# RMSNorm with Swish: the second load goes out from ScalarE's queue beside the first, and gamma's transfer goes behind it

## The chip, the cores and the metric

The kernel runs on one core of a Trainium2 chip. The metric is the device time of one execution in microseconds (us). Most executions of one kernel agree within 0.3%.

A core has 16 DMA engines, which move data between HBM and the on-chip memory. Kernels ask for transfers through queues; this kernel uses two, one issued by SyncE (SP) and one by ScalarE (ACT). In the profile, "SPq" and "ACTq" are the sequencers of those two engines, which issue the transfers; "ACT", "DVE" and "POOL" are the compute engines ScalarE, VectorE and GpSimd.

## The reference

```python
# x: (16, 1024, 512) float32, gamma: (512,), eps = 1e-5
def reference(x, gamma, eps):
    rms = np.sqrt(np.mean(x ** 2, axis=-1, keepdims=True) + eps)
    x_norm = x / rms * gamma
    return (x_norm * (1.0 / (1.0 + np.exp(-x_norm)))).astype(np.float32)
```

That is 16,384 rows of 512 numbers, 33.55 MB in and 33.55 MB out, and little arithmetic for each.

## The kernel before

The rows are cut into tiles of `sz` times 128 rows: each of the 128 partitions takes `sz` rows that lie one after another in HBM, so each partition's part of a load is one contiguous piece of `sz` × 2 KB. The tiles sit in a ring of 96 row slots (25 MB), are worked on in place in chunks of 4 slots, and are stored from there. "Load 0" is the load of the first tile (4 slots, 1 MB), "load 1" the second (4), "load 2" the third (8), "load 3" and later ones 16.

```python
sizes = [4, 4, 8] + [16] * 6 + [8, 8]
ring = 96
ahead = 32
cn = 4
# ...
def load(t):
    nc.sync.dma_start(out=buf(t), in_=dram(xf, t))

def store(t):
    nc.scalar.dma_start(out=dram(of, t), in_=buf(t))
# ... sums(k): squares summed, 3 rows of a chunk on ScalarE, 1 on VectorE
# ... root(k): VectorE, then a power on GpSimd; norm(k): 4 VectorE instructions; swish(k): Silu on ScalarE

with tc.manual_schedule():
    nc.gpsimd.memset(gamma4[:], 0.0)
    nc.gpsimd.memset(neg_half[:], -0.5)
    nc.scalar.dma_start(out=gamma4[0:P:32, :], in_=gamma.partition_broadcast(4))
    nc.scalar.preload_act_table_set("silu_and_others")

    loaded = 0
    rows_loaded = 0
    while rows_loaded < ahead:
        load(loaded)
        rows_loaded += tiles[loaded][1]
        loaded += 1
    # ...
    for k in range(K + 3):
        if k < K:
            sums(k)
            root(k)
        while stored < len(tiles) and ends[stored] <= k - 2:
            store(stored)
            stored += 1
        if k == 0:
            nc.vector.stream_shuffle(gamma_sb[:], gamma4[:], [0] * 32)
        if 1 <= k <= K:
            norm(k - 1)
        if 2 <= k < K + 2:
            swish(k - 2)
            # ... further loads
```

## Time and profile before

| | before |
|---|---|
| time, median | 163.01 us (162.89 to 163.02) |
| span in the profile | 161.1 us |
| moved by DMA | 67.15 MB, 417 GB/s over the span |
| the two queues' packets, share of 16 engines | 49.1% + 48.4% |
| VectorE / ScalarE busy | 69% / 74% |
| ScalarE waits for data, whole run | 23.9 us |

These lines of the page of the kernel before give busy times in us, the DMA total, and the share of the 16 DMA engines' time that each queue's packets took (q1 is SyncE's queue of loads, q10 ScalarE's of stores and gamma):

```profile
DVE 110.7 (69%) x226; ACT 118.7 (74%) x225; POOL 46.4 (29%) x38
DMA packets 3180, 67.15 MB, mean 417 GB/s; under 512 B 356, under 2 KB 356, under 8 KB 360
q1 hardware_dynamic: 1584, 33.56, 49.1%
q10 hardware_dynamic: 1592, 33.56, 48.4%
```

No compute engine is busy as much as three quarters of the time; together the DMA queues are busy 97.5% of it. An average can mix stages, so the windows view of the kernel before is worth a look. Its columns are the stretch, its length, busy time of DVE, ACT and POOL with instruction counts, the clock, the DMA share, and GB/s. A packet, which is one piece that a DMA engine moves at a time, is counted in the stretch in which it starts, so a share can exceed 1:

```profile
0.00:2.00 2.00, 0.00 (x0) 0.00 (x0) 0.77 (x6) 1.00 0.20 25
2.00:3.00 1.00, 0.00 (x0) 0.60 (x1) 0.00 (x0) 1.00 0.62 213
3.00:8.00 5.00, 1.18 (x5) 2.63 (x7) 0.16 (x1) 1.00 1.01 428
8.00:24.00 16.00, 11.03 (x23) 9.62 (x21) 5.17 (x4) 1.00 1.03 431
24.00:100.00 76.00, 67.99 (x140) 72.67 (x140) 28.77 (x20) 1.00 1.00 430
100.00:150.00 50.00, 30.48 (x61) 33.13 (x58) 11.52 (x8) 1.00 1.00 431
150.00:158.00 8.00, 0.00 (x0) 0.00 (x0) 0.00 (x0) 1.00 1.01 432
158.00:161.00 3.00, 0.00 (x0) 0.00 (x0) 0.00 (x0) 1.00 0.13 55
```

From 3 us to 158 us the engines are full, at the same 430 GB/s whether they only load (up to about 20 us), load and store, or only store (the last stretch). Only the first 3 us and the last 3 us have idle DMA time. The compute columns tell the other half: after 150 us nothing computes at all, and stores still drain.

The timeline view of the kernel before shows the start. Its columns are start, length, engine, line and operation, and in brackets the idle time before it and what ended that:

```profile
0.74 23.23 SPq L70 DMA_DIRECT2D xb<-in_x_dram  x8
1.29 1.08 ACTq L116 DMA_DIRECT2D gamma<-in_gamma_dram  x1
...
5.54 0.63 ACT L80 ACTIVATE junk_a<-xb 128x512 bf16<-128x512 f32 x1 [1.85 <-DMA xb<-in_x_dram]
...
8.09 0.63 ACT L80 ACTIVATE junk_a<-xb 128x512 bf16<-128x512 f32 x1 [0.60 <-DMA xb<-in_x_dram]
...
12.98 0.63 ACT L80 ACTIVATE junk_a<-xb 128x512 bf16<-128x512 f32 x1 [2.94 <-DMA xb<-in_x_dram]
...
14.83 1.89 ACT L111 ACTIVATE xb<-xb 128x2048 f32<-128x2048 f32 x1
...
23.70 0.63 ACT L80 ACTIVATE junk_a<-xb 128x512 bf16<-128x512 f32 x1 [3.34 <-DMA xb<-in_x_dram]
```

Loads 0, 1, 2 and 3 reach ScalarE at 5.54, 8.09, 12.98 and 23.70 us, and each time ScalarE was already waiting. Compute is ahead of the data.

### The profile page before, as it was taken

How to read it: one execution, taken by the hardware profiler on the slowest of the kernel's cores; microseconds unless marked ns; L12 is line 12 of the kernel's file. 1: busy time of each engine (PE TensorE's matmuls, PEld its weight loads, DVE VectorE, ACT ScalarE, POOL GpSimd, SP SyncE). 2: the span in 40 equal slices, each digit the busy share in tenths (PEclk: the TensorE clock that was granted, in tenths of full speed). 3: DMA queues.
4: the chain of work that ended last, by engine and by line, in shares of the span. 5: the costliest groups of instructions: out<-in, count | busy, mean ns of one | idle time of the engine just before them, and what ended most of it. 6: DMA issues, size and time to landing. Idle time of an engine off the chain costs nothing.

```text
span 161.1 us, 612 instructions
## 1 busy us (share of the span) xinstructions
DVE 110.7 (69%) x226; ACT 118.7 (74%) x225; POOL 46.4 (29%) x38
## 2 busy tenths in 40 slices
DVE  0376946998999999999966998069999604990000
ACT  3447919999999999999939996099999408954000
POOL 1052403333444433333333333033333302400000
DMA  5999989999899999999999999999999999999993
GB/s 171 437 435 521 390 352 488 413 403 480 366 407 431 484 411 447 399 456 447 399 447 456 399 439 464 417 415 421 431 435 464 419 403 472 415 415 423 439 415 146
DMA packets 3180, 67.15 MB, mean 417 GB/s; under 512 B 356, under 2 KB 356, under 8 KB 360
## 3 DMA queue, kind: packets, MB, share of 16 engines
q1 hardware_dynamic: 1584, 33.56, 49.1%
q10 hardware_dynamic: 1592, 33.56, 48.4%
q14 instruction: 4, 0.03, 0.0%
HBM read 33.56 MB, written 33.55 MB: 417 GB/s over the span
## 4 chain that ended last, share of the span: by engine, by line
DMA 59%; ACT 20%; another core or an unknown queue 4%; issue 4%; DVE 3%; SPq 1%; DVEq 0%; ACTq 0%
DMA xb<-in_x_dram 41%; DMA out_dram<-xb 19%; ACT junk_a L80 12%; ACT xb L111 8%; DVE xb L104 3%; SPq L70 1%; DVEq L178 0%; DVE aeps L93 0%; ACTq L80 0%
## 5 line engine op out<-in xcount | busy, mean ns | idle before, releaser
L104 DVE SCALAR_TENSOR_TENSOR xb<-xb,rstd,gamma_sb 128x512 f32<-128x512 f32 x128 | 87.4, 745 | 0.0
L80 ACT ACTIVATE junk_a<-xb 128x512 bf16<-128x512 f32 x96 | 59.0, 615 | 23.9 <-DMA xb<-in_x_dram 23.9
L97 POOL TENSOR_TENSOR rstd<-aeps,neg_half 128x4 f32<-128x4 f32 x32 | 45.6, 1426 | 94.1 <-DVE aeps L93 94.1
L111 ACT ACTIVATE xb<-xb 128x2048 f32<-128x2048 f32 x32 | 60.7, 1896 | 1.8 <-DVE xb L104 1.8
L86 DVE CUSTOM_DVE_ANT_0 junk_v<-xb 128x512 bf16<-128x512 f32 x32 | 21.9, 685 | 19.6 <-DMA xb<-in_x_dram 19.6
L80 ACT ACTIVATION_READ_ACCUMULATOR junk_a<-xb 128x1 f32 x96 | 18.0, 187 | 0.0
L93 DVE TENSOR_SCALAR aeps<-ms 128x4 f32<-128x4 f32 x32 | 5.4, 170 | 14.5 <-ACT junk_a L80 14.5
L117 ACT ACT_TABLE_LOAD x1 | 1.3, 1283 | 2.4 <-issue 2.4
L86 DVE DVE_READ_ACCUMULATOR2_ANT ms<- 128x1 f32 x32 | 2.6, 82 | 0.0
L140 DVE STREAM_SHUFFLE gamma_sb<-gamma 128x512 f32<-128x512 f32 x1 | 0.7, 725 | 0.0
L114 POOL MEMSET gamma<- 128x512 f32 x1 | 0.5, 524 | 0.3 <-POOLq L164 0.3
L164 POOL MEMSET const-float32-0.0<- 128x1 f32 x1 | 0.1, 98 | 0.2 <-issue 0.2
L164 POOL MEMSET const-bfloat16-1.0<- 128x1 bf16 x1 | 0.1, 101 | 0.0
L164 POOL MEMSET const-uint8-127<- 128x1 uint8 x1 | 0.1, 101 | 0.0
L115 POOL MEMSET neg_half<- 128x4 f32 x1 | 0.1, 101 | 0.0
L164 POOL MEMSET const-float32-1.0<- 128x1 f32 x1 | 0.1, 98 | 0.0
L140 DVE LOAD_MASK_SELECT gamma_sb<-gamma x1 | 0.0, 14 | 0.0
## 6 DMA issues: line engine op xcount, KB each, us to landing
xb<-in_x_dram SPq DMA_DIRECT2D x6, 4096.0 KB, 43.8
out_dram<-xb ACTq DMA_DIRECT2D x6, 4096.0 KB, 34.6
xb<-in_x_dram SPq DMA_DIRECT2D x3, 2048.0 KB, 38.8
out_dram<-xb ACTq DMA_DIRECT2D x3, 2048.0 KB, 13.9
xb<-in_x_dram SPq DMA_DIRECT2D x2, 1024.0 KB, 5.8
out_dram<-xb ACTq DMA_DIRECT2D x2, 1024.0 KB, 19.7
gamma<-in_gamma_dram ACTq DMA_DIRECT2D x1, 8.0 KB
```

Source lines behind the costliest of these rows:

```text
L70: nc.sync.dma_start(out=buf(t), in_=dram(xf, t))
L80: nc.scalar.activation(out=junk[:], in_=row, func=AF.Square, accum_out=ms[:, k, j : j + 1],)
L86: nc.vector.tensor_tensor_reduce(out=junk[:], in0=row, in1=row, scale=1.0, scalar=0.0, op0=ALU.mult, op1=ALU.add, accum_out=ms[:, k, j : j ...
L93: nc.vector.tensor_scalar(out=aeps[:, k, :], in0=ms[:, k, :], scalar1=inv_d, scalar2=eps_f, op0=ALU.mult, op1=ALU.add,)
L97: nc.gpsimd.tensor_tensor(out=rstd[:, k, :], in0=aeps[:, k, :], in1=neg_half[:], op=ALU.pow)
L104: nc.vector.scalar_tensor_tensor(out=row, in0=row, scalar=rstd[:, k, j : j + 1], in1=gamma_sb[:], op0=ALU.mult, op1=ALU.mult,)
L111: nc.scalar.activation(out=rows, in_=rows, func=AF.Silu)
L114: nc.gpsimd.memset(gamma4[:], 0.0)
L115: nc.gpsimd.memset(neg_half[:], -0.5)
L117: nc.scalar.preload_act_table_set("silu_and_others")
L140: nc.vector.stream_shuffle(gamma_sb[:], gamma4[:], [0] * 32)
L164: nc = _bacc.Bacc("TRN2", target_bir_lowering=False, num_devices=1)
```

## The change

The intent is to have two loads under way from the start: SyncE and ScalarE each issue one at the same moment, instead of SyncE issuing both in turn while ScalarE waits for a memset so that it can fetch gamma.

```diff
     def load(t):
-        nc.sync.dma_start(out=buf(t), in_=dram(xf, t))
+        queue = nc.scalar if t == 1 else nc.sync
+        queue.dma_start(out=buf(t), in_=dram(xf, t))
@@
         nc.gpsimd.memset(neg_half[:], -0.5)
-        nc.scalar.dma_start(out=gamma4[0:P:32, :], in_=gamma.partition_broadcast(4))
-        nc.scalar.preload_act_table_set("silu_and_others")
@@
             load(loaded)
             rows_loaded += tiles[loaded][1]
             loaded += 1
+        nc.scalar.dma_start(out=gamma4[0:P:32, :], in_=gamma.partition_broadcast(4))
+        nc.scalar.preload_act_table_set("silu_and_others")
```

## The prediction

> **What bounds the kernel.** The DMA engines. The page counts 67.15 MB moved in a span of 161.1 us. The two hardware queues are busy 49.1% + 48.4% of 16 engines' span, 157.1 us, so 427 GB/s while busy. VectorE is busy 69%, ScalarE 74%. The windows of every 10 us from 24 to 150 us show a DMA share of 0.97 to 1.05; only the first 2.8 us and the last 3 us (share 0.35, then 0.04) are not full. The last store is issued at 146.8 us and lands 13.5 us later, behind a backlog of stores, so compute has several us of slack at the end as well.
>
> **What the change does.** SyncE issues load 0 at 0.74 us (0.37 us), load 1 at 1.16 (0.42), load 2 at 1.63 (0.42). ScalarE issues gamma at 1.29 us (1.09 us), because it waits for GpSimd's memset of that tile, which ends at 1.25; the table load follows at 2.40. After the change, ScalarE should issue load 1 at about 0.74 us, beside load 0, and still reach gamma at about 1.3 and the table load at about 2.4. Load 2 leaves SyncE about 0.45 us earlier. No bytes are added or removed.
>
> The Trainium skill ("DMA: Bandwidth & Descriptors", sections "Issuing engines are not separate DMA queues" and "Queues, rings and completion order") says that both queues run on the same 16 engines, which alternate between them by packet, and that a second issuer saves only issue time. The trace agrees so far: it never holds more than about 430 GB/s with one queue or two. So loads 0 and 1 should not land at about 5.5 and 8.1 us but both near 7.8 us, and gamma just after.
>
> **The critical path, step by step.**
> 1. Start-up: the first packets run from 1.63 us and the engines are full from about 2.8 us. Load 0's issue, which starts this, does not move. Load 1 0.4 us earlier fills nothing, because load 0's packets are not yet through. Worth 0 to -0.3 us; if two simultaneous issues hinder each other, 0 to +0.3.
> 2. First compute: ScalarE's first sum moves from 5.54 to about 7.8 us. Chunk 1's sums then follow chunk 0's without the 0.6 us wait.
> 3. Recovery: before, ScalarE idled 2.94 us until 12.98, for load 2. Cumulative bytes until then are the same, so load 2 still lands near 12.9. Working through VectorE's order with its durations (sum 0.69, shuffle 0.72, four norms 2.73) and the power on GpSimd (1.0 to 1.4), the first norms end near 14.7 rather than 12.9, and the first Silu starts at 14.8 to 15.3 instead of 14.83. Whatever is left is absorbed by the 3.3 us wait for load 3 (23.70 us).
> 4. Load pacing: completion semaphores are reused in program order, so gamma's later place makes SyncE's sixth load wait for load 1, the seventh for load 2 and the eighth for gamma: issued near 8, 13 and 13 us instead of 5.5, 8.0 and 23.6. SyncE's queue holds over 8 MB throughout, so this moves no byte.
>
> So a delay of about 2.3 us for the first data, all off the critical path; net about -0.1 us.
>
> **Prediction:** 162.9 us, range 162.4 to 163.6. Faster by over 2%: 0.01; within 2%: 0.98; slower: 0.01.
>
> **What would show it right:** ScalarE's first sum at 7.5 to 8.1 us; load 2 and load 3 first used at 13.0 and 23.7, within 0.3; last loads first used near 133.7; mean rate 417 GB/s again. **Wrong if** load 0 still lands near 5.5 us (the queues are not shared evenly), if the DMA windows before 3 us differ clearly, or if a store leaves so late that a DMA window drops below 0.9.

## The result, and the profile after

The changed kernel takes 163.13 us (median of 4 executions, 163.06 to 163.27), the kernel before 163.01. The ratio is 1.001, with a 95% interval of 0.9993 to 1.0027: the same. Here and below, a ratio is the mean time of one kernel's runs over the mean of the other's in the same rounds, so it is not quite the ratio of the medians quoted. Executions over 1.5% slower than the fastest of the same kernel are left out of the means.

These are the same lines of the page after the change:

```profile
DVE 110.6 (69%) x226; ACT 118.6 (74%) x225; POOL 46.4 (29%) x38
DMA packets 3180, 67.15 MB, mean 416 GB/s; under 512 B 356, under 2 KB 356, under 8 KB 360
q10 hardware_dynamic: 1736, 34.61, 50.0%
q1 hardware_dynamic: 1440, 32.51, 47.6%
```

One megabyte has moved from q1 to q10; the sum is the same. The timeline view after the change:

```profile
0.74 0.41 ACTq L71 DMA_DIRECT2D xb<-in_x_dram  x1
0.74 23.08 SPq L71 DMA_DIRECT2D xb<-in_x_dram  x7
1.29 1.08 ACTq L124 DMA_DIRECT2D gamma<-in_gamma_dram  x1
...
8.01 0.63 ACT L81 ACTIVATE junk_a<-xb 128x512 bf16<-128x512 f32 x1 [4.33 <-DMA xb<-in_x_dram]
...
13.04 0.63 ACT L81 ACTIVATE junk_a<-xb 128x512 bf16<-128x512 f32 x1 [1.25 <-DMA xb<-in_x_dram]
...
14.89 1.89 ACT L112 ACTIVATE xb<-xb 128x2048 f32<-128x2048 f32 x1
...
23.56 0.63 ACT L81 ACTIVATE junk_a<-xb 128x512 bf16<-128x512 f32 x1 [3.13 <-DMA xb<-in_x_dram]
```

Both first loads are indeed issued at 0.74 us. The first sum then starts 2.47 us *later* than before (8.01 against 5.54), because two transfers that share the engines both finish when the second would have. That delay is gone six microseconds later: load 2 is in use at 13.04 us (12.98 before), the first Silu starts at 14.89 (14.83), load 3 is in use at 23.56 (23.70). It was taken out of ScalarE's wait for load 2, which shrinks from 2.94 to 1.25 us, and out of the idle gap between chunks 0 and 1.

The windows view after the change, for the stretches in which it could differ:

```profile
0.00:2.00 2.00, 0.00 (x0) 0.00 (x0) 0.77 (x6) 1.00 0.37 66
2.00:3.00 1.00, 0.00 (x0) 0.60 (x1) 0.00 (x0) 1.00 0.67 180
3.00:8.00 5.00, 0.00 (x0) 0.68 (x1) 0.00 (x0) 1.00 1.00 423
8.00:24.00 16.00, 12.27 (x27) 11.61 (x27) 5.34 (x4) 1.00 1.02 430
24.00:100.00 76.00, 68.11 (x140) 72.52 (x140) 28.80 (x20) 1.00 1.00 429
```

Multiplying GB/s by length, the bytes moved by 3 us are 0.312 MB after against 0.263 MB before, a lead worth 0.1 us at 430 GB/s. By 8 us they are 2.43 against 2.40 MB, and by 24 us 9.31 against 9.30 MB. In this trace the second queue gives the engines a few more packets at the start and changes nothing that lasts. The lead itself is hardly larger than the scatter: the same sums give 0.20 to 0.26 MB by 3 us in three traces that issue loads 0 and 1 in turn on one queue, and 0.24 to 0.31 MB in four that issue them at one moment on two.

### The profile page after: what moved, and what is told of

Its sections match the earlier page's. It is cut to its first block, busy times and chain, and to the rows that moved or that the text cites. A ratio compares the mean times of both kernels' runs of the same rounds, so it can differ in the third digit from the quotient of the medians.

```text
span 161.4 us, 611 instructions
## 1 busy us (share of the span) xinstructions
DVE 110.6 (69%) x226; ACT 118.6 (74%) x225; POOL 46.4 (29%) x38
## 4 chain that ended last, share of the span: by engine, by line
DMA 40%; ACT 39%; another core or an unknown queue 4%; issue 4%; DVE 3%; SPq 0%; DVEq 0%; ACTq 0%
DMA xb<-in_x_dram 40%; ACT junk_a L81 22%; ACT xb L112 17%; DVE xb L105 3%; SPq L71 0%; DVEq L179 0%; DVE aeps L94 0%; ACTq L81 0%
## 5 line engine op out<-in xcount | busy, mean ns | idle before, releaser
L87 DVE CUSTOM_DVE_ANT_0 junk_v<-xb 128x512 bf16<-128x512 f32 x32 | 21.9, 685 | 21.0 <-DMA xb<-in_x_dram 21.0
```

The costliest lines, as they stand in the source:

```text
L87: nc.vector.tensor_tensor_reduce(out=junk[:], in0=row, in1=row, scale=1.0, scalar=0.0, op0=ALU.mult, op1=ALU.add, accum_out=ms[:, k, j : j ...
```

## The experiments

The theory is that the time is set by DMA occupancy: once the 16 engines are full, the finish follows from the bytes left, and data that reach compute late cost nothing as long as the engines don't run dry. The main rival is that two effects cancel, a gain at the start from the second queue and a loss from the late first sums. A second rival is that the arrival of the first data counts by itself. All runs gave correct results except the two "light" ones. The four runs of each group used one chip and shared the runs of the kernel before: 163.15 us in the first group, 163.06 in the second, 163.10 in the third.

### The change again

Edit: none; the changed kernel itself.

> The change itself once more, to bound its effect. Theory (the 16 DMA engines are full either way, so first data that come 2.4 us later cost nothing): 163.0 to 163.2 us, ratio to before 0.999 to 1.002. Rival (a gain at the start and a loss from the late first sums cancel): the same here; the next run tells them apart.

163.45 us, ratio 1.0016 (1.0003 to 1.0029). By itself this looks like a small real loss. The same kernel in the third group had an expectation for that:

> The change a third time: 1.0010 and 1.0016 of before so far. If it really costs 0.1 to 0.3 us, the ratio is again above 1.0005; if that was chance of the executions, it lies on either side of 1.000, within 0.001.

162.94 us, ratio 0.9991 (0.9979 to 1.0004). The three ratios are 1.0010, 1.0016 and 0.9991, so even the sign differs from group to group, and the groups ran on different chips. As times, the three are +0.16, +0.26 and −0.15 us, and their intervals reach from −0.34 to +0.47. The effect, if there is one, is smaller than this method can fix.

### Half of the change: gamma later, load 1 still on SyncE's queue

```diff
# against the changed kernel
-        queue = nc.scalar if t == 1 else nc.sync
+        queue = nc.sync
```

> Half of the change: gamma issued later in program order, load 1 still on SyncE's queue. ScalarE's queue holds nothing else before it, so its issue should stay at about 1.3 us. Theory: first sum at 5.5 us, time 163.0 within 0.2. A rival that puts the absence of an effect down to gamma (its earlier place helping or hindering the first loads by some tenths) expects a shift of 0.2 us or more.

163.13 us, ratio 1.0001 (0.9987 to 1.0014). The trace has gamma's issue at 1.29 us as before. Gamma's place neither helps nor hinders.

### The other half: load 1 on ScalarE's queue, gamma still ahead of it

```diff
-        nc.sync.dma_start(out=buf(t), in_=dram(xf, t))
+        queue = nc.scalar if t == 1 else nc.sync
+        queue.dma_start(out=buf(t), in_=dram(xf, t))
```

> The other half of the change: load 1 on ScalarE's queue, but gamma still ahead of it, so that load 1 is issued only at about 2.4 us, after gamma's 1.09 us issue. Load 0 then has a start of about 1.6 us alone and should land earlier than in the changed kernel, at 5.8 to 6.9 us, load 1 near 8.0 to 9. Time by the theory: 163.0 within 0.3, as the DMA engines are full from load 0 and load 2 alone.

163.06 us, ratio 0.9995 (0.9979 to 1.0011): the time is as expected. The landing of load 1 is not. The timeline and, last, two lines of the page's list of DMA issues (KB each, median us from issue to landing) of this run:

```profile
2.45 0.36 ACTq L71 DMA_DIRECT2D xb<-in_x_dram  x1
5.79 0.63 ACT L81 ACTIVATE junk_a<-xb 128x512 bf16<-128x512 f32 x1 [2.09 <-DMA xb<-in_x_dram]
...
15.67 0.63 ACT L81 ACTIVATE junk_a<-xb 128x512 bf16<-128x512 f32 x1 [7.94 <-DMA xb<-in_x_dram]
...
xb<-in_x_dram SPq DMA_DIRECT2D x1, 1024.0 KB, 5.0
xb<-in_x_dram ACTq DMA_DIRECT2D x1, 1024.0 KB, 13.1
```

Load 1 was expected near 8 to 9 us and arrived at 15.6: a megabyte took 13.1 us. The packet records, which the packed trace holds for every packet with its queue, size, start and length, explain it in three parts. First, its packets only began at 6.80 us, 4.35 us after the issue, when SyncE's queue had long been full, and behind gamma's, which began at 5.50. Second, the engines then took packets from the two queues in turn, one from each, and those of load 1 are 8 KB while those of loads 2 and 3 are 16 and 32 KB. Third, the 4-byte record that reports a load's completion took its turn too: the last data of load 1 ended at 13.90 us, these records ran from 14.70 to 15.11, about the length of one 32 KB packet (1.2 us) later. My expectation had shared the engines by bytes. The next run puts that to a harder test.

### Load 3 on ScalarE's queue in place of load 1

```diff
-        queue = nc.scalar if t == 1 else nc.sync
+        queue = nc.scalar if t == 3 else nc.sync
```

> The changed kernel, but it is load 3 (16 rows) that goes out on ScalarE's queue at the start, and loads 0, 1, 2 on SyncE's. If the queues share the engines evenly by packet, loads 0, 1, 2 land near 8, 13 and 23 us instead of 5.5, 8 and 13, and load 3 near 22 to 24. So chunks 2 and 3 start 10 us later than before. Theory: the stretch of waits at 84, 104 and 133 us takes that up; 163.0 to 163.8 us. If the slack of the compute engines is smaller than about 7 us: 165 us or more.

163.26 us, ratio 1.0006 (0.9991 to 1.0021). The time is as the theory expects, but the landings again miss: the expectation says "by packet", yet its landing times are those of equal shares in bytes. The timeline and two lines of the list of DMA issues of this run:

```profile
15.72 0.63 ACT L81 ACTIVATE junk_a<-xb 128x512 bf16<-128x512 f32 x1 [12.04 <-DMA xb<-in_x_dram]
...
xb<-in_x_dram ACTq DMA_DIRECT2D x1, 4096.0 KB, 15.1
xb<-in_x_dram SPq DMA_DIRECT2D x2, 1024.0 KB, 16.0
```

Load 0 was expected near 8 us and is used at 15.72. A load of 4 MB and a load of 1 MB, issued together, finished together. Each engine has eight packets of each, one per partition it serves; they are 32 KB and 8 KB long, and in the records they took 1,213 ns and 309 ns (medians). Eight such pairs are 8 × 1.522 = 12.2 us, which after a start-up of about 2.7 us gives 14.9: close to the 15.1 us from issue to landing plus 0.74. So the queues take turns by packet, and a packet here is as long as the contiguous piece.

For the main question this is the better run for having missed. The first sum is 10.2 us late, four times as late as in the change, and the time has not moved by a measurable amount. ScalarE's waits for data fall from 23.9 us to 15.6, of which 12.0 are the first one: after 24 us it waits for no data at all, so its spare time later in the run is used up.

### One load of 8 rows in place of two of 4

```diff
-    sizes = [4, 4, 8] + [16] * 6 + [8, 8]
+    sizes = [8, 8] + [16] * 6 + [8, 8]
```

> Before, with the first two loads of 4 rows made one of 8 rows: one queue, no second issuer, but first data as late as in the changed kernel. Theory: first sum at 7.9 to 8.2 us, time 163.0 plus or minus 0.3. Rival (cancelling): the loss without the gain, so slower by as much as the second queue gains, 0.3 to 0.6 us (163.3 to 163.6), or by up to 2.4 us if first data were all that counts.

163.56 us, ratio 1.0028 (1.0016 to 1.0041), and the first sum at 8.73 us, later than the 7.9 to 8.2 expected. This is 0.4 us slower, inside the rival's range of 163.3 to 163.6, so on its own it speaks for the rival. The next two pairs of runs were made to decide it.

### No compute to hide anything: both kernels with sums, roots and norms left out

```diff
         if k < K:
-                sums(k)
-                root(k)
+                pass
...
         if 1 <= k <= K:
-                norm(k - 1)
+                pass
```

> Wrong results on purpose: sums, roots and norms are left out, only Silu on the raw rows remains, so compute can't be late. Theory: the DMA engines still set the time; 162.3 to 163.0 us. If compute set part of the time before, clearly less: below 161.

> The same cut on the changed kernel. Theory: no gain from the second queue at the start, so within 0.2 us of the run light_before. Rival (a start-up gain of 0.3 to 0.6 us hidden by the late first sums): faster than light_before by 0.3 us or more, since here no late sums can hide it.

The cut kernel before takes 162.21 us (ratio 0.9939, 0.9923 to 0.9956), the cut changed kernel 162.0 to 162.45 in four executions (ratio 0.9946, 0.9930 to 0.9963); two more of its executions were at over 169 us, and are left out. Their means are 162.22 and 162.27 us. The hidden gain of 0.3 us or more, which the cancelling rival needs, does not show. With 0.2 us of scatter among the executions the difference of the means is uncertain by about 0.3 us, so this pair alone puts a gain of that size at the edge of what it can exclude; the lead of at most about 0.1 us in the bytes moved speaks against it too. Note also how little all of the sums and norms are worth: 0.9 us out of 163. The windows view shows a difference at the very end. These are the last stretches of the kernel before, and then of the same kernel cut:

```profile
158.00:159.00 1.00, 0.00 (x0) 0.00 (x0) 0.00 (x0) 1.00 0.35 148
159.00:160.00 1.00, 0.00 (x0) 0.00 (x0) 0.00 (x0) 1.00 0.04 16
```

```profile
158.00:159.00 1.00, 0.00 (x0) 0.00 (x0) 0.00 (x0) 1.00 0.50 213
159.00:160.00 1.00, 0.00 (x0) 0.00 (x0) 0.00 (x0) 1.00 0.00 0
```

In both, all engines are full to 158 us; then some still have packets and others have none. By the packet records the last packet ends at 159.88 us before and at 159.30 in the cut kernel, which is the whole difference of the two profiled spans (161.1 and 160.5 us). So in these traces even this small gain lies in how unevenly the engines finish, not in compute that was waited for in between. Why the finish is shorter isn't shown.

### The same late data, but the engines start late too

```diff
         nc.gpsimd.memset(neg_half[:], -0.5)
+        nc.gpsimd.memset(xb[:, 0:4, :], 0.0)      # load 0 must wait for this
```

> Before, with a memset on GpSimd of the rows of the first load (about 2.1 us, estimated from 0.52 us for 512 elements), so that the first load is issued at about 3.4 us instead of 0.74 and everything on SyncE's queue behind it. First data at about 8.2 us, as in the changed kernel, but the DMA engines start late as well. Theory: 163.0 + 2.6 = 165.6 us, within 0.4. Rival (only when data first reach the compute engines counts): the changed kernel's 163.1.

165.40 us, ratio 1.0137 (1.0123 to 1.0151). The timeline of this run:

```profile
1.23 1.80 POOL L116 MEMSET xb<- 128x2048 f32 x1
...
3.06 7.62 SPq L70 DMA_DIRECT2D xb<-in_x_dram  x7
7.87 0.63 ACT L80 ACTIVATE junk_a<-xb 128x512 bf16<-128x512 f32 x1 [4.18 <-DMA xb<-in_x_dram]
```

This is the decisive pair with the change. Both have their first sum at about the same time, 7.87 here and 8.01 there. There the engines were already full, and it cost nothing measurable. Here the first load is issued 2.32 us later (3.06 against 0.74; the memset took 1.80 us instead of the 2.1 estimated), the engines stand idle for that long, and the time rises by 2.25 us. The rival that counts arrival of first data expected 163.1 and falls.

### How late may the first data be?

```diff
-    sizes = [4, 4, 8] + [16] * 6 + [8, 8]
+    sizes = [16] + [16] * 6 + [8, 8]      # first16
+    sizes = [32] + [16] * 5 + [8, 8]      # first32
+    sizes = [48] + [16] * 4 + [8, 8]      # first48
```

> Before, with the loads of 4, 4 and 8 rows made one of 16 rows on SyncE's queue, to measure the slack: first data at about 13.0 us (where 16 rows had landed before), 7.4 us late. Theory: the DMA engines stay full, 162.9 to 163.5 us. A rival with a slack of only a few us (the 2.4 us of the change being just inside it) expects 166 us or more.

> The same with one first load of 32 rows: first data at about 23 us, 17.5 us late. ScalarE's 117 us of work from there end at about 140 us at the earliest, still before the 146.8 us at which the last Silu ends before. Theory: the ring of 96 rows takes loads until about 61 us, and the first store, issued at about 55 us, comes before that, so the DMA engines stay full: 162.9 to 164.5 us. Rival (slack of 10 to 15 us): 166 to 171 us.

> The same with 48 rows: first data at about 32 us; the first store can be issued only after 12 chunks of 3.64 us, at about 78 us, but the ring is full of loaded rows at about 61 us. Theory: this makes a hole of about 16 us in which the DMA engines have nothing to do, and the hole is paid in full: 175 to 183 us, with a DMA share near 0 between about 61 and 77 us. A rival for which lateness of first data is what counts, whether or not the engines run dry, expects a smooth rise from first16 over first32 to here.

| first tile | first sum at, us | time, us | ratio to before (95%) |
|---|---|---|---|
| 4 rows (before) | 5.54 | 163.01 | |
| 4 + 4 together (the change) | 8.01 | 163.13 | 1.0010 (0.9993 to 1.0027) |
| 8 rows | 8.73 | 163.56 | 1.0028 (1.0016 to 1.0041) |
| 16 rows | 13.03 | 163.91 | 1.0056 (1.0040 to 1.0071) |
| load 3 beside load 0 | 15.72 | 163.26 | 1.0006 (0.9991 to 1.0021) |
| 32 rows | 22.72 | 163.06 | 1.0007 (0.9976 to 1.0039) |
| 48 rows | 32.80 | 185.98 | 1.1402 (1.1387 to 1.1418) |

The first data may be 17 us late, and the time does not follow. With 32 rows the first store is issued at 56.79 us, while loads still run, and the engines stay full. Then, with first data 10 us later, the time jumps by 23 us. The windows of the run with 48 rows show what happened:

```profile
50.00:60.00 10.00, 9.66 (x22) 10.00 (x19) 4.31 (x3) 1.00 1.00 430
60.00:65.00 5.00, 4.63 (x10) 5.00 (x14) 1.44 (x1) 1.00 0.04 15
65.00:81.00 16.00, 15.07 (x31) 16.00 (x30) 6.89 (x5) 1.00 0.00 0
81.00:82.00 1.00, 1.00 (x3) 1.00 (x4) 0.30 (x1) 1.00 0.00 0
82.00:84.00 2.00, 1.79 (x6) 2.00 (x5) 0.50 (x1) 1.00 0.93 393
```

The ring of 96 rows is full of loaded data when the last packet of a load ends at 61.7 us. The first store is issued at 81.41 us, and its first packet starts at 82.34. In between the DMA engines have nothing to do; by the shares that is 4.8 + 16 + 1 + 0.1 = 21.9 us of idle time, and the run is 22.9 us longer. My estimate of the hole, 16 us, was too small: it put the first store at 78 us and its packets right after the issue. The mechanism was as expected, and the price is the hole.

What doesn't fit is the small print. 8 and 16 rows came out 0.3% and 0.6% slower, with intervals that exclude zero, and 16 rows went past the 163.5 us allowed. Lateness alone doesn't order them, since 15.72 us shows less than 8.73 and 13.03, and 22.72 no more. The executions with a tile of 32 rows spread from 162.60 to 164.17 us, and the profiled one, the slowest of these, has a DMA share of 0.12 from 159 to 160 us and 0.04 from 160 to 161, where the kernel before has 0.04 and 0.00: one or two of the 16 engines finish last, a microsecond later than there. Such an uneven finish may be what moves these times. Whether it explains the 8- and 16-row results was not shown; the profiled execution with 16 rows happened to be its fastest, 163.35 us. In the profiled executions the last packet ends at 160.29 us with 8 rows and 160.19 with 16, against 159.88 before, but in three of the change it ends anywhere from 159.83 to 160.50. That stays open.

No version with correct results came out clearly faster than both kernels: about 155 us of full transfer, a start of 3 us or more and an uneven finish are common to all of them.

## Why the prediction was right

The time, 163.13 us, lies in the range of 162.4 to 163.6, and the class "within 2%" was right. Point by point:

1. *"What bounds the kernel. The DMA engines."* Right, and shown by experiment: taking away nearly all of VectorE's work and half of ScalarE's gained 0.9 us, 2.32 us of later issue cost 2.25 us, and a hole of 21.9 us cost 22.9.
2. *"Load 1 0.4 us earlier fills nothing."* Right to within what can be measured. "Nothing" was too strong: in the first 2 us the DMA share rose from 0.20 to 0.37. But the lead at 3 us was 0.05 MB, worth 0.1 us, no larger than the scatter among traces, and was gone in noise by 24 us. The same step has the first packets at 1.63 us; in the trace they start at 1.74. The forecast net of −0.1 us is neither confirmed nor refuted, as three comparisons gave +0.10%, +0.16% and −0.09%.
3. *"Loads 0 and 1 should ... land ... both near 7.8 us."* Right: both were there when the first sum started at 8.01, within the 7.5 to 8.1 allowed. The Trainium skill, "DMA: Bandwidth & Descriptors", section "Issuing engines are not separate DMA queues", says that transfers from different issuers run on the same 16 engines and interleave, and that a second issuer saves only issue time. This trace agrees: 428 GB/s with one queue of loads (3 to 8 us before) and 423 with two (after). But equal shares of the time, and so the landing together, hold only because both loads have 8 KB packets, which was luck. The prediction says "by packet"; my later expectations reckoned with equal bytes for other sizes all the same, and two runs showed that the shares are equal in packets.
4. *Recovery.* Right in each number: first norms ended at 14.63 us (forecast 14.7), the first Silu started at 14.89 (14.8 to 15.3), load 2 was in use at 13.04 (13.0), load 3 at 23.56 (23.7 within 0.3). The last loads were used at 133.08 rather than near 133.7, which changed nothing.
5. *"Load pacing: ... the seventh for load 2 and the eighth for gamma."* Wrong, without consequence. The waits of SyncE's queue after the change have this line:

```profile
SPq L71 <- DMA gamma<-in_gamma_dram: 0.8, 1, 0.8
```

It was the seventh load that waited for gamma and went out at 9.3 us, and the eighth still waited for load 3, until 23.5 us. I had taken the reuse of completion semaphores to follow the program's order strictly; the trace shows gamma's as the third in the rotation, not the fifth. As the prediction said, no byte moved for it.

## What to carry to other kernels

Ask first whether the engines that set the time are ever idle: here a gap in DMA work has a price of about one microsecond per microsecond, and the arrival of the first data has none that follows its lateness until the ring fills and nothing can be stored (the 0.3% and 0.6% of two versions stay unexplained). With the DMA engines full, as here, issuing a load from a second queue didn't add speed; it only decided who finishes first, and the load that compute needs next may finish later. If you do put two loads side by side, mind that the queues took turns by packet here, so the one with the shorter contiguous pieces gets the smaller share.

## What the Trainium skill lacked or had wrong

- "DMA: Bandwidth & Descriptors", "Queues, rings and completion order", says that an engine drains a packet of typically 9 to 17 descriptors from one queue before it turns to the next. It doesn't say what this means for shares. In the packet records here the turns were single contiguous pieces of 8, 16 or 32 KB, where a turn of nine would have moved all eight pieces that an engine has of the 1 MB load, so that of two loads issued together the one of 1 MB was in use after 14.98 us and the one of 4 MB landed after 15.1 us.
- No page has it that a queue which gets work after the other has filled must wait: gamma's first packet came at 5.54 us after an issue at 1.29 before the change, load 1's at 6.80 after 2.45 when it was issued alone on ScalarE's queue behind gamma, and the first store's at 20.93 after 16.76 before the change. With nothing in the other queue the wait was 1.4 and 0.9 us: gamma's first packet came at 2.68 after 1.29 in the run with the late first load, and the first store's at 82.34 after 81.41 with 48 rows. Issued at the same moment as load 0, at 0.74 us, load 1's first packet came at 2.08. What holds the later queue back isn't shown.
- "DMA: Bandwidth & Descriptors", "Specifications", gives about 358 GB/s per core as the limit of HBM and 435 as the fabric's. In this one-core program the trace holds 430 GB/s over 126 us, so the sentence under "Where 436 GB/s comes from" that the HBM side binds for transfers between HBM and on-chip memory doesn't hold for it. The same page's measured 425 GB/s for a core that streams alone agrees.
- No page gives the size of the uneven finish: before the change all 16 engines are full to 158 us, and the share is 0.35 and then 0.04 in the next two microseconds, with the last packet ending at 159.88 us; in the slowest profiled execution with a first tile of 32 rows it is 0.62, 0.12 and 0.04 in three.
- No page gives the time until the engines are full: the first load's issue starts at 0.74 us, its first packet at 1.74, and only from about 3 us is the share 1.
